# Summing gathered weights with two 64-column products per token, and a last scaling that reads its norm from PSUM

## The chip, the cores and the metric

The kernel runs on one core of a Trainium2 chip. A core has five engines that run side by side and meet at semaphores: PE (TensorE, matrix products, with its weight loads PEld), DVE (VectorE), ACT (ScalarE), POOL (GpSimd) and SP (SyncE, which here only issues transfers). Data come from HBM into SBUF by DMA; PE writes its results into PSUM. The metric is the time of one execution on the device in microseconds (us), lower is better.

## The reference, cut to what matters

One layer of a decoder trunk is run on 512 prompt tokens and 64 sample tokens (D = 2048). After a mixer come eight heads of a product-key lookup ("PEER"): for every token and head the best 16 of 16384 small experts are chosen, and their outputs are summed with weights.

```python
top, pos = lax.top_k(cand, PEER_TOPK)
eidx = jnp.take_along_axis(cidx, pos, axis=-1)
g = jax.nn.softmax(top, axis=-1)
act = jax.nn.gelu(jnp.einsum('td,thkd->thk', xb, expert_u[eidx])) * g
out = jnp.einsum('thk,thkd->td', act, expert_v[eidx])
...
x = x + gate2 * out
y = rmsnorm(x, final_g)        # x / sqrt(mean(x^2) + eps) * final_g
```

The outputs are y for both groups of tokens and the recurrent states of the mixer.

## The kernel before

**Stages.** The first 960 us hold the mixer; then come the queries, keys and choices of the experts. From 1207 us on the kernel walks through the experts themselves. Each expert number is a pair (row, column) of a 128x128 grid. The 80 rows of the grid that are chosen most (`L = 80`) are done densely for all 512 prompt tokens; picks in the other rows are fetched one row of 8 KB at a time with indirect DMAs ("gathers") and dotted on VectorE.

**The u stage (L1645 to L1722).** It has 160 halves, `n = 0..159`, two for each dense row. `u_half` (L1388) issues 24 products of 128x128 weights with 512 columns (L1398). ACT and POOL have split the weights into a high and a low part before (`xhi` L925, `xlo` L926), from `raw` tiles that SP loads some halves ahead. Among these the loop places, for each half, what belongs to the rest: a few gathers of u rows (POOL L1234) with their dot products (DVE L1262, whose second operand `hT` lies in PSUM), steps of the choice, and, from about n = 54 on, the weights' table.

**The weights' table ("Gather's sums").** The dense part needs, for each token, the 128 columns by 80 rows of its softmax weights. For four tokens (`b`) `g_pair` (DVE L1585) makes, per token, two one-hot matrices over the token's 128 picks: `op` (128 picks x 128 columns, scaled by ACT in `g_scale`, L1593) and `wr` (128 picks x 80 rows). `g_mm` (L1595) multiplies the two on PE, so that each token's sum of weights stands in PSUM as 128x80. `g_out` (ACT L1606) copies four tokens out to `stg`, and for each 32 tokens four transfers of 320 KB (`gd<-stg`, POOL L1611) bring it to HBM. `g_eight` (L1632) does two `b` at a time, into the banks `gbank` and `gx`: 64 such blocks in all. One stands either before a `u_half` (odd n) or in its middle (`mid`, even n). Nothing else of PE runs inside a block. In `g_mm` each token's 128 output partitions are cut into four slices of 32, each a product of its own on 32 columns of the array.

**The order.** The engines run in the order in which the code issues (`manual_schedule`); each engine has one queue.

**The v stage and the end.** From 2240 us on the dense v rows are multiplied (L1421, `v_column`), and gathered v rows are added (DVE L1290). The last group adds, per chunk k of 16 (128 channels x 512 tokens), the gathered tokens by four transposing products (L1425), then `v_sum` (L1438) scales by `gate2` on DVE (L1445), squares on ACT (L1449), stores a copy (`x2d`, SP L1450) and adds the squares on DVE (L1455). After k = 15 `token_norm` (L1457) sums the squares on PE (L1463), takes the root (`rstd`, L143 to L149), and spreads the result over the partitions with PE into the PSUM bank `prfa` (L1468); ACT copies it to SBUF as `R` (L1470). Then the 16 chunks are scaled by `R` and `final_g` (L1811 to L1819): 11 on DVE in one operation, 5 (k = 2, 5, 8, 11, 14) first on ACT, then on POOL. SP stores each chunk to `y`. A fallback (L1825 on) follows that runs only when a count overflows.

Of the kernel before, what the change touches and what calls it, by code (L numbers as in the profile page):

```python
# [9 lines left out]
AF = mybir.ActivationFunctionType  # L10
ALU = mybir.AluOpType
# [5 lines left out]
KD = 16  # L17
# [13 lines left out]
NA = NP  # L31
NG = T - NA
NE = 128
L = 80
# [38 lines left out]
C_FG = 232  # L73
# [7 lines left out]
def build(ctx, tc, A, O, dbg=None):  # L81
    nc = tc.nc
    V, S, PE, G = nc.vector, nc.scalar, nc.tensor, nc.gpsimd
# [11 lines left out]
    cols = const.tile([128, C_ALL], F32, name="cols")  # L95
# [117 lines left out]
    def square_sum(src, k, st, nm):  # L213

        if k == 0:
            st.append(wk.tile([128, T], F32, name=f"sqa_{nm}", tag="R", bufs=1))
            S.activation(st[0], src, AF.Square)
# [7 lines left out]
    def norm_stats(st, n, nm):  # L225
# [7 lines left out]
        def spread():  # L233
            out = nm != "n1" and wk.tile([128, T], F32, name=f"R_{nm}", tag="R", bufs=1)
            pr = [pst.tile([128, 512], F32, name=f"st_{nm}_{i}", tag="st") for i in range(2)]
            for i in range(4):
                PE.matmul(pr[0][:, i * 128:(i + 1) * 128], c[:, 0, i:i + 1].to_broadcast([128, 128]), ident,
                          start=True, stop=True)
            PE.matmul(pr[1][:, :64], c[:, 0, 4:5].to_broadcast([128, 128]), ident[:, 64:], start=True, stop=True)
            if nm == "n1":  # L240
                return pr[0], pr[1][:, :64]
            S.activation(out[:, :NP], pr[0], AF.Copy)
            S.activation(out[:, NP:], pr[1][:, :64], AF.Copy)
            return out
# [19 lines left out]

    def modulate(src, R, jscale, jshift, k0, nk, nm):

        sc, sh = mods[jscale], mods[jshift]
        for k in range(k0, k0 + nk):
            m = wk.tile([128, NP], F32, name=f"m_{nm}_{k}", tag="sq", bufs=2)
            hi, lo = hv[0][:, k, :NP], hv[1][:, k, :NP]  # L270
            if R is None:
                V.tensor_scalar(m, src[:, k, :NP], sc[:, k, 0:1], sh[:, k, 0:1], op0=ALU.mult, op1=ALU.add)
                S.activation(hi, src[:, k, :NP], AF.Identity, scale=sc[:, k, 0:1], bias=sh[:, k, 0:1])
                (G if k % 2 else V).tensor_sub(lo, m, r32(hi))
            else:
                V.tensor_mul(m, src[:, k, :NP], R[:, :NP])
                S.activation(hi, m, AF.Identity, bias=sh[:, k, 0:1])
                V.scalar_tensor_tensor(lo, m, sh[:, k, 0:1], r32(hi), op0=ALU.add, op1=ALU.subtract)
        kk = slice(k0, k0 + nk)
        m = wk.tile([128, nk, NB * NS], F32, name=f"ms_{nm}_{k0}", tag="ms", bufs=1)  # L280
        eng = V if R is None else G
        if R is None:
            V.tensor_tensor(s4(m), s4(src[:, kk, NP:T]), ctx_b(sc, kk), op=ALU.mult)
        else:
            eng.tensor_mul(m, src[:, kk, NP:T], R[:, None, NP:T].to_broadcast([128, nk, NB * NS]))
        eng.tensor_tensor(s4(m), s4(m), ctx_b(sh, kk), op=ALU.add)
        split(hv[0][:, kk, NP:T], hv[1][:, kk, NP:T], m, eng)
# [47 lines left out]
    for hc in range(4):  # L335
# [11 lines left out]
        for kq in range(4):  # L347
# [3 lines left out]
            if hc == 0 and kq == 0:  # L351
                R = spread()
# [213 lines left out]
    for i in range(KW):  # L566
# [6 lines left out]
        if i == 0:  # L573
            R = spread()
# [18 lines left out]
    R = spread()  # L593
# [33 lines left out]
    R = spread()  # L627
# [226 lines left out]
    for i in range(RB):  # L854
        r, k = new_row(f"row0_{i}")
# [522 lines left out]
    fin = {}  # L1378
# [55 lines left out]
    def add_x(q, kq):  # L1434
        k = 4 * q + kq
        V.scalar_tensor_tensor(acc[:, k, :], acc[:, k, :], g2[:, k, 0:1], fin["x", q][:, kq, :], op0=ALU.mult, op1=ALU.add)

    def v_sum(gi, k, pv):  # L1438
        ak = acc[:, k, :]
        if gi == 0:  # L1440
            S.activation(ak, pv, AF.Copy)
        elif gi < len(GROUPS) - 1:
            V.tensor_add(ak, ak, pv)  # L1443
        else:
            V.scalar_tensor_tensor(ak, pv, g2[:, k, 0:1], ak, op0=ALU.mult, op1=ALU.add)  # L1445
            if k == 0:
                fin["t"] = [actp.tile([128, NA], F32, name=f"sqs{i}", tag="act") for i in range(3)]
            sq = fin["t"][1]
            S.activation(sq, ak, AF.Square)  # L1449
            nc.sync.dma_start(x2d[:, k, :], ak)  # L1450
            if k == 0:
                fin["sq"] = fin["t"][0]
                V.tensor_copy(fin["sq"], sq)
            else:
                V.tensor_add(fin["sq"], fin["sq"], sq)  # L1455

    def token_norm(sq, n, nm, pool, banks):  # L1457

        nt = -(-n // 128)
        w = min(128, n)  # L1460
        pc, pr = banks
        for i in range(nt):
            PE.matmul(pc[:w, i:i + 1], sq[:, i * 128:i * 128 + w], ones[:, 0:1], start=True, stop=True)  # L1463
        c = pool.tile([128, 3, nt], F32, name=f"rcf{nm}")
        rstd(c[:w, 0, :], pc[:w, :nt], D, c[:w, 1, :], c[:w, 2, :])
        yield
        for i in range(nt):
            PE.matmul(pr[:, i * 128:i * 128 + w], c[:w, 0, i:i + 1].to_broadcast([w, 128]), ident[:w, :w], start=True, stop=True)  # L1468
        R = fin["t"][2] if nm == "a" else pool.tile([128, n], F32, name=f"Rf{nm}")
        S.activation(R, pr[:, :n], AF.Copy)  # L1470
        yield
        return R

# [121 lines left out]
    def g_mm(b, pg):  # L1595
        ops, wr, j0 = pair.pop(b)
        for j in range(4):
            for a in range(0, 128, 32):
                PE.matmul(pg[a:a + 32, j * L:(j + 1) * L], ops[:, j0 + j, a:a + 32], wr[:, j0 + j, :],  # L1599
                          start=True, stop=True)  # L1600

    def g_out(b, pg):
# [121 lines left out]
    vp = ctx.enter_context(tc.tile_pool(name="vp", bufs=1, side="right"))  # L1724
    acc = vp.tile([128, KD, NA], F32, name="acc")
# [39 lines left out]
    for m in range(M):  # L1765
        gi, q, bl, first, final = steps[m]
        n = NU2 + 2 * m
# [12 lines left out]
        for kq in range(KD // VQ):  # L1780
# [9 lines left out]
            k, pv = v_column(n, gi, q, bl, first, final, kq)  # L1790
# [9 lines left out]
    def drive(gen):  # L1800
        while True:
            try:
                next(gen)
            except StopIteration as e:
                return e.value

    def norm_banks(nm):
        return pbank("u", f"pcf{nm}", 2), pbank("g", f"prf{nm}", 2)

    R = drive(token_norm(fin["sq"], NA, "a", vp, norm_banks("a")))  # L1810
    for k in range(KD):  # L1811
        ak = acc[:, k, :]
        fg = cols[:, C_FG + k:C_FG + k + 1]
        if k % 3 == 2:
            S.activation(ak, ak, AF.Copy, scale=fg)
            G.tensor_mul(ak, ak, R)
        else:
            V.scalar_tensor_tensor(ak, ak, fg, R, op0=ALU.mult, op1=ALU.mult)
        nc.sync.dma_start(O["y"][:, k, :NA], ak)  # L1819


    epx.close()
# [2 lines left out]
    with tc.If(any_ > 0), tc.tile_pool(name="fb", bufs=1) as fp:  # L1825
        io1 = fp.tile([128, 128], F32, name="f_io1")
        V.tensor_scalar(io1, iota, 1.0, None, op0=ALU.add)
        for i, (p0, n, c) in enumerate(GT):
# [19 lines left out]
            a = fp.tile([128, D], F32, name=f"f_a{i}", tag="a", bufs=1)  # L1848
# [33 lines left out]
        R = drive(token_norm(sqs, NA, "f", fp, norm_banks("f")))  # L1882
# [72 lines left out]
```

## Time and profile before

| | us |
|---|---|
| median of 3 runs (lowest, highest) | 3210.41 (3208.57, 3221.06) |
| the profiled execution's own time | 3213.08 |
| its span, first to last instruction | 3211.3 |
| PE / DVE / POOL / ACT busy | 3042.5 / 2228.9 / 1796.5 / 1041.5 |
| bytes moved by DMA | 881.12 MB |

The profile is of one execution. Its rows name a line of the kernel, an engine, an operation, what it writes and reads (out<-in), and how often it ran; then busy time, mean duration in ns, and idle time just before it with the releaser that ended most of it. "PE" rows are matrix products, "PEld" rows the loads of their weights. An fp32 product of the program appears as two pairs of records, one load and one product each: `g_eight` has 32 products, and 64 product records in the trace. "SPq" and the like are the issuing of transfers, not their movement.

### The profile page before, as it was taken

To read this page: it belongs to the slowest core of one execution; us is meant where nothing else is said; L and a number is where in the kernel's file an instruction comes from. 1 tells how busy PE (TensorE), PEld (TensorE's weight loads), DVE (VectorE), ACT (ScalarE), POOL (GpSimd) and SP (SyncE) were. 2 spreads that over 40 slices of the span, in tenths; PEclk is the share of its full clock that TensorE was granted. 3 is DMA by queue.
4 is the path that set the end of the run, shared out by engine and by line. 5 is a ranking of instruction groups with operands and counts; after the bars stand their busy time and mean duration, and the time that the engine had idled before them with its cause. 6 is when DMAs were issued, how large, how long until landed. Compare 5 with 4: busy or idle time off the path is not lost.

```text
span 3211.3 us, 52705 instructions
## 1 busy us (share of the span) xinstructions
PE 3042.5 (95%) x20313; PEld 2569.5 (80%) x20313; DVE 2228.9 (69%) x3296; ACT 1041.5 (32%) x1645; POOL 1796.5 (56%) x1097
## 2 busy tenths in 40 slices
PE   5999999999989999999999999999999999999997
PEld 2688798899979998886777777777887778777776
DVE  5356521234356797988899888877679898878955
ACT  3243311123232223232665555542322222222222
POOL 2233233344333335665676676777777778777842
PEclk8999999999989999999999999999999999999998
DMA  9833465633332226989889998998999998999964
GB/s 373 295 136 135 163 216 204 210 115 117 130 134 101 70 77 216 314 323 358 331 303 341 358 385 324 396 369 341 392 411 411 410 377 299 374 384 360 378 202 144
DMA packets 251057, 881.12 MB, mean 274 GB/s; under 512 B 36230, under 2 KB 37126, under 8 KB 194342
## 3 DMA queue, kind: packets, MB, share of 16 engines
q0 software_dynamic: 78096, 475.29, 37.5%
q1 hardware_dynamic: 161760, 382.48, 33.8%
q10 hardware_dynamic: 10944, 19.93, 1.6%
q8 instruction: 160, 2.62, 0.3%
q14 instruction: 97, 0.79, 0.1%
HBM read 878.84 MB, written 65.76 MB: 294 GB/s over the span
## 4 chain that ended last, share of the span: by engine, by line
PE 76%; DMA 10%; DVE 6%; issue 4%; POOL 2%; ACT 1%; SPq 0%; POOLq 0%; DVEq 0%; ACTq 0%
PE pu L1398 24%; PE pv L1421 17%; PE pp_o L139 6%; DMA raw<-vq 3%; PE pp_s L139 3%; PE pp_c L139 3%; PE pp_x L139 3%; PE qb L139 3%; PE pp_b L139 3%; DMA v<-v,rows 2%; PE ada L189 2%; PE pp_y L139 2%; PE qa L139 2%; DMA wa<-w_ada 2%; PE gx L1599 2%
## 5 line engine op out<-in xcount | busy, mean ns | idle before, releaser
L926 POOL TENSOR_TENSOR xlo<-raw,xhi 128x1024 fp32r<-128x1024 f32 x320 | 785.5, 2464 | 395.9 <-ACT xhi L925 391.5
L1262 DVE SCALAR_TENSOR_TENSOR u<-u,hT 128x2048 f32<-128x2048 f32 x223 | 504.9, 2283 | 142.1 <-DMA u<-u,rows 124.0
L925 ACT ACTIVATE xhi<-raw 128x1024 fp32r<-128x1024 f32 x320 | 338.3, 1060 | 760.0 <-PE pv L1421 282.8
L1290 DVE SCALAR_TENSOR_TENSOR accB<-v,dots,accB 128x2048 f32<-128x2048 f32 x211 | 496.4, 2352 | 124.1 <-DMA v<-v,rows 120.4
L1421 PE MATMUL pv<-ahi,xhi 128*128 128x512 f32 x1280 | 507.0, 396 | 30.6 <-DVE acc L1443 26.7
L1398 PE MATMUL pu<-hhi,xhi 128*128 128x512 f32 x1280 | 507.4, 396 | 0.7 <-ACT qt L949 0.7
L1398 PE MATMUL pu<-hhi,xlo 128*128 128x512 f32 x1280 | 499.3, 390 | 6.3 <-POOL xlo L926 6.3
L1421 PE MATMUL pv<-alo,xhi 128*128 128x512 f32 x1280 | 503.4, 393 | 1.1 <-DVE alo L1372 1.1
L1421 PE MATMUL pv<-ahi,xlo 128*128 128x512 f32 x1280 | 503.3, 393 | 0.1
L1398 PE MATMUL pu<-hlo,xhi 128*128 128x512 f32 x1280 | 499.2, 390 | 0.0
L1421 PEld LDWEIGHTS pv<-ahi,xhi 128*128 128x128 f32 x1280 | 243.8, 190 | 85.9 <-issue 16.0
L1234 POOL DMA_INDIRECT v<-v,rows x223 | 260.5, 1168 | 63.2 <-issue 44.8
L1398 PEld LDWEIGHTS pu<-hhi,xlo 128*128 128x128 f32 x1280 | 240.6, 188 | 58.6 <-POOL xlo L926 7.5
L1398 PEld LDWEIGHTS pu<-hhi,xhi 128*128 128x128 f32 x1280 | 240.5, 188 | 57.6 <-issue 1.7
L1421 PEld LDWEIGHTS pv<-ahi,xlo 128*128 128x128 f32 x1280 | 243.3, 190 | 52.4 <-POOL xlo L926 1.0
L1421 PEld LDWEIGHTS pv<-alo,xhi 128*128 128x128 f32 x1280 | 244.0, 191 | 51.5 <-DVE alo L1372 1.5
L1234 POOL DMA_INDIRECT u<-u,rows x223 | 226.8, 1017 | 97.2 <-DVE u L1262 46.2
L1398 PEld LDWEIGHTS pu<-hlo,xhi 128*128 128x128 f32 x1280 | 240.9, 188 | 47.8
L1593 ACT ACTIVATE op<-op,it 128x128 f32<-128x128 f32 x512 | 155.2, 389 | 0.0
L128 POOL TENSOR_TENSOR wlo_q<-raw_q,whi_q 128x1024 fp32r<-128x1024 f32 x28 | 68.7, 2456 | 147.1 <-ACT whi_q L126 147.1
L189 PE MATMUL ada<-wa,cpad 128*32 128x512 f32 x768 | 109.8, 669 | 40.6 <-DMA wa<-w_ada 40.6
L1401 ACT ACTIVATE act<-pu 128x512 f32<-128x512 f32 x80 | 47.9, 598 | 295.3 <-PE pu L1398 291.1
(506 smaller groups left out, 5687.2 us busy)
## 6 DMA issues: line engine op xcount, KB each, us to landing
wa<-w_ada SPq DMA_DIRECT2D x96, 1024.0 KB
raw<-ut SPq DMA_DIRECT2D x160, 512.0 KB
raw<-vq SPq DMA_DIRECT2D x320, 256.0 KB
gd<-stg POOLq DMA_DIRECT2D x64, 320.0 KB
gsb<-gd POOLq DMA_DIRECT2D x20, 1024.0 KB
actd<-act ACTq DMA_DIRECT2D x76, 256.0 KB
actr<-actd POOLq DMA_DIRECT2D x19, 1024.0 KB
raw_o<-w_out SPq DMA_DIRECT2D x32, 512.0 KB
```

The costliest lines, as they stand in the source:

```text
L128: lo_engine(share).tensor_sub(lo, raw, r32(hi))
L139: PE.matmul(o, st, mv[pick](k), start=first, stop=last)
L189: PE.matmul(acc[32 * g:32 * g + 32, :], cpad[:, 4 * kq + g, :], w[:, g, :], start=kq == 0, stop=kq == 3)
L925: S.activation(hi, raw, AF.Copy)
L926: G.tensor_sub(lo, raw, r32(hi))
L1234: G.indirect_dma_start(out=out, out_offset=None, in_=src, in_offset=bass.IndirectOffsetOnAxis(ap=idx, axis=0), bounds_check=NE * 128 - 1, ...
L1262: V.scalar_tensor_tensor(r, r, 1.0, st["h"], op0=ALU.mult, op1=ALU.mult, accum_out=dots[i][:, j:j + 1])
L1290: V.scalar_tensor_tensor(st["a"], r, dots[i][:, j:j + 1], st["a"], op0=ALU.mult, op1=ALU.add)
L1398: PE.matmul(pu, st[:, kk, :], movA[mv](k), start=k == 0 and a == 0, stop=k == KD - 1 and a == 2)
L1421: PE.matmul(pv, st, mv, start=first and j == 0 and a == 0, stop=last and not end and j == SG - 1 and a == 2)
L1593: S.activation(ops[:, j0 + j, :], ops[:, j0 + j, :], AF.Copy, scale=it[2][:, b * 4 + j:b * 4 + j + 1])
L1599: PE.matmul(pg[a:a + 32, j * L:(j + 1) * L], ops[:, j0 + j, a:a + 32], wr[:, j0 + j, :], start=True, stop=True)
```

## The change

Three edits. First, `g_mm` cuts the 128 output partitions of a token into two slices of 64, not four of 32: two products per token on 64 columns of the array each, with the same 80 moving columns. Second, the five chunks that POOL scales at the end are now k = 1, 4, 7, 10, 13, and ACT multiplies them by `final_g` inside `v_sum`, three chunks after each is complete (two for k = 13). Third, `R` is copied from PSUM by DVE, not ACT; DVE's own 11 chunks read the norm straight from the PSUM bank, and only POOL reads the copy; ACT's queue, not SP's, stores POOL's five chunks.

```diff
+    scaled_early = (1, 4, 7, 10, 13)
     def v_sum(gi, k, pv):
...
                 V.tensor_add(fin["sq"], fin["sq"], sq)
+            e = k - 2 if k == KD - 1 else k - 3
+            if e in scaled_early:
+                S.activation(acc[:, e, :], acc[:, e, :], AF.Copy, scale=cols[:, C_FG + e:C_FG + e + 1])
...
         R = fin["t"][2] if nm == "a" else pool.tile([128, n], F32, name=f"Rf{nm}")
-        S.activation(R, pr[:, :n], AF.Copy)
+        if nm == "a":
+            V.tensor_copy(R, pr[:, :n])
+        else:
+            S.activation(R, pr[:, :n], AF.Copy)
...
         for j in range(4):
-            for a in range(0, 128, 32):
-                PE.matmul(pg[a:a + 32, j * L:(j + 1) * L], ops[:, j0 + j, a:a + 32], wr[:, j0 + j, :],
+            for a in range(0, 128, 64):
+                PE.matmul(pg[a:a + 64, j * L:(j + 1) * L], ops[:, j0 + j, a:a + 64], wr[:, j0 + j, :],
                           start=True, stop=True)
...
-    R = drive(token_norm(fin["sq"], NA, "a", vp, norm_banks("a")))
+    banks = norm_banks("a")
+    R = drive(token_norm(fin["sq"], NA, "a", vp, banks))
     for k in range(KD):
         ak = acc[:, k, :]
-        fg = cols[:, C_FG + k:C_FG + k + 1]
-        if k % 3 == 2:
-            S.activation(ak, ak, AF.Copy, scale=fg)
+        if k in scaled_early:
             G.tensor_mul(ak, ak, R)
+            nc.scalar.dma_start(O["y"][:, k, :NA], ak)
         else:
-            V.scalar_tensor_tensor(ak, ak, fg, R, op0=ALU.mult, op1=ALU.mult)
-        nc.sync.dma_start(O["y"][:, k, :NA], ak)
+            V.scalar_tensor_tensor(ak, ak, cols[:, C_FG + k:C_FG + k + 1], banks[1][:, :NA], op0=ALU.mult, op1=ALU.mult)
+            nc.sync.dma_start(O["y"][:, k, :NA], ak)
```

The first place is PE's queue around the first block of the table, in the u stage. Before, each bank takes 16 products with weights of 32 columns:

```order
L1398 MATMUL pu_14112<-hlo,xhi_13977 128x512
L1398 MATMUL pu_14112<-hhi,xlo_13978 128x512
L1599 MATMUL gbank<-wr_13884,op_13883 32x80 x16
L1599 MATMUL gx_14125<-wr_13884,op_13883 32x80 x16
L1398 MATMUL pu_14112<-hhi,xhi_13977 128x512
```

Now it takes 8 with 64 columns, at the same place:

```order
L1398 MATMUL pu_14112<-hlo,xhi_13977 128x512
L1398 MATMUL pu_14112<-hhi,xlo_13978 128x512
L1607 MATMUL gbank<-wr_13884,op_13883 64x80 x8
L1607 MATMUL gx_14125<-wr_13884,op_13883 64x80 x8
L1398 MATMUL pu_14112<-hhi,xhi_13977 128x512
```

Nothing around the blocks moves on any engine: the block has half as many products.

The second place is ACT's queue at the end of the program, from the last weight splits (`xhi`) on. `sqs` is the square of a chunk, `rcfa` the column of norms, `acc` the chunks. Before:

```order
L925 ACTIVATE xhi_29536<-raw_29332 128x1024
L1449 ACTIVATE sqs_29360<-acc 128x512 x8
L144 ACTIVATE rcfa<-rcfa 128x4
L1470 ACTIVATE sqs_29361<-prfa 128x512
L1815 ACTIVATE acc<-acc,cols 128x512 x5
L1823 TENSOR_LOAD flag
```

Now:

```order
L925 ACTIVATE xhi_28514<-raw_28308 128x1024
L1451 ACTIVATE sqs_28336<-acc 128x512 x3
L1460 ACTIVATE acc<-acc,cols 128x512
L1451 ACTIVATE sqs_28336<-acc 128x512 x3
L1460 ACTIVATE acc<-acc,cols 128x512
L1451 ACTIVATE sqs_28336<-acc 128x512 x2
L1460 ACTIVATE acc<-acc,cols 128x512
L144 ACTIVATE rcfa<-rcfa 128x4
L1824 DMA y<-acc 128x512 x5
L1831 TENSOR_LOAD flag
```

The five scalings by `final_g` have gone from behind the root (L144) to between the squares, the copy of `R` has left ACT, and five stores have come to its queue. DVE has the copy in its place, ahead of its 11 chunks:

```order
L149 TENSOR_TENSOR rcfa<-rcfa 128x4
L1476 COPY sqs_28337<-prfa 128x512
L1826 SCALAR_TENSOR_TENSOR acc<-acc,cols,prfa 128x512 x11
L1831 TENSOR_LOAD flag
```

SP's queue keeps 11 of its 16 stores of `y`.

## The prediction

> **What bounds the kernel now.** I read the page first: busy shares, then the chain that ended last.
>
> ```profile
> PE 3042.5 (95%) x20313; PEld 2569.5 (80%) x20313; DVE 2228.9 (69%) x3296; ACT 1041.5 (32%) x1645; POOL 1796.5 (56%) x1097
> PE 76%; DMA 10%; DVE 6%; issue 4%; POOL 2%; ACT 1%; SPq 0%; POOLq 0%; DVEq 0%; ACTq 0%
> ```
>
> PE is busy for 95% of the span and is 76% of the chain; what shortens PE's own work shortens the kernel, as long as nobody else becomes late. "issue", 4%, is waiting that no other engine explains. The change works in two stretches, so I asked for windows: the stretch with the weights' table (1527 to 2140 us), the v stage, and one with the densest transfers.
>
> ```profile
> core 0: us, PE busy (x) PEld busy (x) DVE busy (x) ACT busy (x) POOL busy (x), PEclk, DMA share, GB/s
> 1527.00:2140.00 613.00, 594.06 (x6223) 473.23 (x6223) 529.34 (x727) 349.24 (x769) 427.59 (x308) 1.00 0.91 349
> 2240.00:3100.00 860.00, 828.11 (x3599) 680.42 (x3598) 712.71 (x400) 205.40 (x192) 649.53 (x407) 0.98 0.94 367
> 2027.00:2077.00 50.00, 48.35 (x495) 38.47 (x494) 40.56 (x39) 27.92 (x62) 35.28 (x26) 1.00 1.02 413
> ```
>
> In the table's stretch PE idles 613.00 - 594.06 = 18.9 us, at full granted clock (1.00). The groups by line of that stretch say where:
>
> ```profile
> L1599 PE MATMUL gx<-wr,op 128*32 128x80 f32 x2048 | 65.3, 234 | 18.9 <-issue 18.9
> L1599 PE MATMUL gbank<-wr,op 128*32 128x80 f32 x2048 | 48.7, 236 | 0.0
> ```
>
> All idle time of PE here stands ahead of products into `gx`, the second bank of a block, none ahead of `gbank`, the first. The two banks get the same 2048 products, yet `gx` takes 65.3 + 18.9 = 84.2 us and `gbank` 48.7. PE's rows in order of time show two of the 64 blocks:
>
> ```profile
> 1874.30 0.76 PE L1599 MATMUL gbank<-wr,op 128*32 128x80 f32 x32
> 1874.88 0.74 PE L1599 MATMUL gx<-wr,op 128*32 128x80 f32 x18
> 1876.01 0.35 PE L1599 MATMUL gx<-wr,op 128*32 128x80 f32 x4 [0.39 <-issue]
> 1876.76 0.35 PE L1599 MATMUL gx<-wr,op 128*32 128x80 f32 x5 [0.40 <-issue]
> 1877.53 0.36 PE L1599 MATMUL gx<-wr,op 128*32 128x80 f32 x5 [0.42 <-issue]
> 1877.81 0.50 PE L1398 MATMUL pu<-hhi,xhi 128*128 128x512 f32 x1
> ...
> 1886.20 0.76 PE L1599 MATMUL gbank<-wr,op 128*32 128x80 f32 x32
> 1886.78 0.74 PE L1599 MATMUL gx<-wr,op 128*32 128x80 f32 x32
> 1887.44 0.50 PE L1398 MATMUL pu<-hhi,xhi 128*128 128x512 f32 x1
> ```
>
> The later block is clean: 64 products in 1.24 us. The earlier one runs at the same pace for 32 + 18 = 50 products and then gets only four or five every 0.75 us, so that it takes 3.51 us. The many small products outrun something that feeds PE or takes its records away. The trace does not name it; it shows when it bites: late in a block, never within the first 32 products (the idle time 0.0 of `gbank` covers all 64 blocks). The earliest I found:
>
> ```profile
> 1586.18 0.76 PE L1599 MATMUL gbank<-wr,op 128*32 128x80 f32 x32
> 1586.76 0.45 PE L1599 MATMUL gx<-wr,op 128*32 128x80 f32 x12
> ```
>
> Here 44 went through, then came a pause. The 3.51 us block starts 0.77 us after POOL issued a transfer of the table:
>
> ```profile
> 1873.53 0.92 POOL L1611 DMA_DIRECT2D gd<-stg  x1
> ```
>
> **The change part by part.** *Stalls in the blocks.* A clean `gx` half is 0.74 us, so 64 of them are 47.4; they took 84.2, so stalls cost 84.2 - 47.4 = **36.8 us**. After the change a block has 32 product records, not 64: as many as the half that never stalls. I take all 36.8 as removed. The bounds are 0 (what feeds PE is slow for a time, not after a count) and 36.8.
>
> *The clean block.* Does it get shorter or longer? Eight groups of four slices fill `gbank` in 1886.78 - 1886.20 = 0.58 us, 0.072 us a group. The nearest rows for a stream in fp32 are the transposing products near the end, and for weight loads with next to no stream the sums of squares:
>
> ```profile
> 3172.85 1.05 PE L1425 MATMUL pv<-ident,tok 128*128 128x128 f32 x8
> 3172.62 1.08 PEld L1425 LDWEIGHTS pv<-ident,tok 128*128 128x128 f32 x8
> ...
> 3187.13 0.97 PEld L1463 LDWEIGHTS pcfa<-ones,sqs 128*128 128x128 f32 x8 [2.54 <-issue]
> ```
>
> Less a tail of some 0.2 us, eight products with 128 moving columns come every 0.11 us; 80 columns scale to 0.069. So a group of four slices takes what one slice's stream takes: the slices run side by side and the stream is the limit. Two slices of 64 stream the same 80 columns in as many groups (8 a bank), so the block keeps its 1.24 us. The load doubles in columns. L1463 loads 128 columns every 0.112 us ((0.97 - 0.19)/7, 0.19 being one load), so 64 take 0.056, less than the stream's 0.069, and L1425 shows a load of 0.11 lying wholly beside a stream of 0.11. I take 0 for the clean block; the bounds are 0 and the slower rival's price, below.
>
> [...] So the saving lies in the stalls.
>
> *What lies beside.* With 36.8 us less, the stretch lasts 576 us, and the others must do their work in it. DVE's 529.3 us are 92% of that. DMA moved 349 GB/s x 613 us = 214 MB, which needs 371 GB/s; the window at 2027 us held 413. What DVE and SP's loads waited for in this stretch:
>
> ```profile
> DVE u L1262 <- DMA u<-u,rows: 74.7, 53, 4.9
> ...
> SPq L909 <- POOL xlo L926: 529.4, 90, 9.0
> ```
>
> SP's loads wait for buffers to come free, not for bandwidth, so they have slack; DVE's 74.7 us of waiting for gathered rows say that gathers are near their limit in places. If DMA can't rise above the 0.94 of the v stage, the stretch shrinks only to 613 x 0.91 / 0.94 = 593, and 17 of the 36.8 are given back. If the 1.02 of the dense window holds, nothing is. Nearer to the latter, as that is the same stage: I take **5 us given back**, bounds 0 and 17.
>
> *The end.* After the last products, in order of time:
>
> ```profile
> 3184.82 0.75 DVE L1445 SCALAR_TENSOR_TENSOR acc<-pv,mod,acc 128x512 f32<-128x512 f32 x1 [1.43 <-PE pv L1425]
> 3185.66 0.63 ACT L1449 ACTIVATE sqs<-acc 128x512 f32<-128x512 f32 x1 [2.99 <-DVE acc L1445]
> ...
> 3191.81 0.60 ACT L1470 ACTIVATE sqs<-prfa 128x512 f32<-128x512 f32 x1 [3.19 <-PE prfa L1468]
> 3192.30 3.16 ACT L1815 ACTIVATE acc<-acc,cols 128x512 f32<-128x512 f32 x5
> 3192.44 12.46 DVE L1818 SCALAR_TENSOR_TENSOR acc<-acc,cols,sqs 128x512 f32<-128x512 f32 x11 [2.81 <-ACT sqs L1470]
> 3193.09 7.94 POOL L1816 TENSOR_TENSOR acc<-acc,sqs 128x512 f32<-128x512 f32 x5 [29.82 <-ACT acc L1815]
> 3193.22 13.53 SPq L1819 DMA_DIRECT2D y<-acc  x16
> ```
>
> DVE's 11 chunks set the pace of the stores. Groups of two short windows, with POOL at work and without it, and a group of an operation with one input in PSUM:
>
> ```profile
> L1818 DVE SCALAR_TENSOR_TENSOR acc<-acc,cols,sqs 128x512 f32<-128x512 f32 x4 | 6.8, 1760 | 0.0
> ...
> L1818 DVE SCALAR_TENSOR_TENSOR acc<-acc,cols,sqs 128x512 f32<-128x512 f32 x5 | 3.4, 740 | 0.0
> ...
> L1262 DVE SCALAR_TENSOR_TENSOR u<-u,hT x223: 2269/2283/2291, 1250.7 to 2203.5; 128x2048 f32<-128x2048 f32 x112
> ```
>
> With both tensor inputs in SBUF a chunk takes 1760 ns beside POOL and 740 alone. L1262, whose `hT` lies in PSUM, spreads by only 22 ns over 223 runs, though POOL works through much of that time. So with the norm in PSUM all 11 run at about 3.4/5 = 0.68 us: 7.5 us, not 12.46, and DVE ends 5.0 us earlier. The stores don't keep up with that:
>
> ```profile
> 3193.00:3203.00 10.00, 0.00 (x0) 0.00 (x0) 10.00 (x9) 2.46 (x5) 7.94 (x5) 0.50 0.57 208
> 3203.00:3208.00 5.00, 0.00 (x0) 0.00 (x0) 1.90 (x3) 0.00 (x0) 0.00 (x0) 0.50 1.03 381
> ```
>
> The 16 x 256 KB = 4.19 MB need 11.0 us at 381 GB/s. Begun at 3194.3, a microsecond after the first issue, they land by 3205.3; before, 2.08 and 1.90 MB had gone by 3208, and the rest landed at about 3208.6. Gain 3.3 us. DVE's copy of the norm starts where ACT's 0.60 us did and is bounded by that and the 0.75 of L1445; 0.1 more than ACT's. **The end: 3.2 us**, bounds 0 and 5.0. The five early scalings cost ACT 0.63 each (3.16/5) inside gaps of 2.99 us ahead of its squares: nothing, as long as the stored copy of a chunk has been read within the two or three chunks (7 us or more) before ACT overwrites it; were it late, ACT's next square and DVE behind it would wait, and PE for a bank.
>
> *The sum.* 3213.08 - 36.8 + 5 - 3.2 = 3178.1 for the profiled execution. The median of the runs is 2.7 below it: **3175 us**.
>
> **The rivals.** *The load is not hidden (slower).* [...] As a mechanism of this kernel: if the two 64-column loads of a group run neither beside each other nor beside the streams, a group takes 2 x 0.056 + 0.069 = 0.181 us, not 0.072, and 16 groups in 64 blocks add 112 us: 3210.4 + 112 - 36.8 - 3.2 = 3282. It decides once a group takes over 0.13 us. Against it: four 32-column loads fit into 0.072 us now, and L1425's load lies beside its stream. 5%.
>
> *The stall is one of time.* If the feed turns slow some 0.77 us into a block whatever has run, half as many products wait half as long: 18.4 us saved, 3189. For it: pauses follow transfers of the table. Against it: in the rows above they come after 44 and 50 products, and in `gbank` never. 10%.
>
> *DMA takes over.* At a share of 0.94, 17 us are given back: 3210.4 - 36.8 + 17 - 3.2 = 3187; DVE would then wait more for `u` rows. 10%.
>
> *It doesn't do what it says.* The stalls have another cause and stay: 3207. 7%.
>
> **How the numbers follow.** My forecast has 68%, with 3166 to 3184 of its own (all bounds at their best: 3210.4 - 36.8 - 5.0 = 3169, and 3 for the runs' spread). To leave out no more than 2 in 10, the range reaches to the second and third rivals: 3166 to 3192. About 0.5%, 16 us, is what a measurement of this kernel can tell from no change; 3194 is that line. Forecast, time and DMA rivals lie below it: 0.87 with some loss to spread; stalls that stay lie within: 0.08; slower 0.05.
>
> **What would show it.** In the new profile `gx` has 1024 product records, each with 64 columns, no idle time, and the same busy time as `gbank`; a block takes about 1.24 us; PE's idle time in the stretch is near 0. DVE's chunks at the end take 740 ns beside POOL, and the last window shows DMA near 380 GB/s from its start. Wrong would be: blocks of 2 us or more without pauses (the load), pauses that begin before the 32nd product (time), or new waits of PE for `xlo` in the u stage (DMA).

## The result, and the profile after

The new kernel takes **3182.57 us** (median of 4 runs, 3180.04 to 3183.95), the kernel before beside it 3209.68 (4 runs, 3208.57 to 3221.06): a ratio of 0.9907, with a 95% interval from 0.9892 to 0.9921. The forecast was 3175, between 3166 and 3192. The profiled execution took 3181.82 us, its span is 3179.9.

On other chips, used for the experiments, the kernel before was not always that slow. This turned out to be the main finding, so it stands first:

| where | kernel before, median (runs) | pauses in its blocks | with the change |
|---|---|---|---|
| first occasion (chip not recorded) | 3209.68 (4) | yes | 3182.57, the new kernel |
| chip 10 | 3185.30 (23) | no | 3183.97, its products alone |
| chip 0 | 3185.97 (17) | no | 3180.36, the new kernel |
| chip 12 | 3209.19 (7) | yes | 3178.89, a variant of the new kernel |
| chip 15 | 3213.35 (1) | yes | not run |

Whether there are pauses is read from traces: on chip 0 of the kernel before itself, on chips 10, 12 and 15 of kernels with the same narrow products. The page, and the window that showed 18.9 us of idle PE before:

```profile
PE 3026.1 (95%) x18265; PEld 2566.4 (81%) x18265; DVE 2217.7 (70%) x3297; ACT 1040.1 (33%) x1644; POOL 1793.6 (56%) x1097
...
1527.00:2140.00 613.00, 610.04 (x4290) 495.52 (x4289) 541.59 (x732) 355.08 (x770) 448.01 (x323) 1.00 0.93 365
```

PE has 2048 product records fewer (20313 to 18265) and is busy for 610.04 of 613 us, not 594.06. The groups of PE over all 64 blocks (1520 to 2110 us):

```profile
L1607 PE MATMUL gbank<-wr,op 128*64 128x80 f32 x1024 | 49.9, 239 | 0.0
L1607 PE MATMUL gx<-wr,op 128*64 128x80 f32 x1024 | 46.8, 233 | 0.0
```

Both banks now take about 48 us and nothing is idle ahead of either. Together that is 96.7 us, where it was 48.7 + 65.3 + 18.9 = 132.9. One block in order of time:

```profile
2085.56 0.78 PE L1607 MATMUL gbank<-wr,op 128*64 128x80 f32 x16
2086.16 0.72 PE L1607 MATMUL gx<-wr,op 128*64 128x80 f32 x16
2086.82 0.50 PE L1398 MATMUL pu<-hhi,xhi 128*128 128x512 f32 x1
```

It lasts 2086.82 - 2085.56 = 1.26 us; a clean one lasted 1.24 before. In 0.60 us 16 products start in a bank, where it was 32 in 0.58.

The end, from DVE's last sum on, in order of time, and two windows (columns as before):

```profile
3155.80 0.75 DVE L1447 SCALAR_TENSOR_TENSOR acc<-pv,mod,acc 128x512 f32<-128x512 f32 x1 [1.42 <-PE pv L1425]
...
3163.15 0.69 DVE L1476 COPY sqs<-prfa 128x512 f32<-128x512 f32 x1 [2.23 <-PE prfa L1473]
3163.76 7.32 DVE L1826 SCALAR_TENSOR_TENSOR acc<-acc,cols,prfa 128x512 f32<-128x512 f32 x11
3163.92 6.17 POOL L1823 TENSOR_TENSOR acc<-acc,sqs 128x512 f32<-128x512 f32 x5 [28.83 <-DVE sqs L1476]
```

```profile
3163.00:3168.00 5.00, 0.11 (x1) 0.00 (x0) 4.85 (x8) 0.00 (x0) 4.08 (x4) 0.50 0.55 202
3168.00:3173.00 5.00, 0.00 (x0) 0.00 (x0) 3.08 (x5) 0.00 (x0) 2.09 (x2) 0.50 1.04 379
```

DVE's 11 chunks take 7.32 us, not 12.46, although POOL works beside them for 6.17; from 3168 us on the stores run at 379 GB/s, and they end the work: DVE is done at 3171.1 us, the last of their packets at 3177.4.

Where the 31.4 us between the two profiled spans come from, by the starts of the first and the last block and of DVE's last sum:

| stretch | before | after | difference |
|---|---|---|---|
| up to the first block | 1527.05 | 1523.77 | -3.3 |
| first block to last block | 610.4 | 575.6 | -34.8 |
| last block to DVE's last sum | 1047.3 | 1056.4 | +9.1 |
| DVE's last sum to the end | 26.5 | 24.1 | -2.4 |

The rows are 1527.05 and 2137.48 (`gbank`) and 3184.82 before, 1523.77, 2099.40 and 3155.80 after. The first stretch is before anything that changed; over all fourteen profiled executions of these kernels the first block starts between 1520.2 and 1528.8 us, so -3.3 is scatter. What was given back, 9.1, has a place of its own. The waits of POOL and of PE between 2090 and 2240 us, just behind the blocks, before:

```profile
POOL gsb L1345 <- DMA gd<-stg: 9.8, 1, 9.8
PE pu L1398 <- POOL xlo L926: 4.2, 1, 4.2
```

and after:

```profile
POOL gsb L1345 <- DMA gd<-stg: 10.2, 1, 10.2
PE pu L1398 <- POOL xlo L926: 9.9, 3, 7.0
```

Rows of POOL and then PE, in order of time, after:

```profile
2137.67 1.04 POOL L1234 DMA_INDIRECT u<-u,rows  x1 [0.16 <-issue]
2148.88 0.56 POOL L1345 DMA_DIRECT2D gsb<-gd  x1 [10.16 <-DMA gd<-stg]
2149.45 2.36 POOL L926 TENSOR_TENSOR xlo<-raw,xhi 128x1024 fp32r<-128x1024 f32 x1
...
2151.87 0.79 PE L1398 MATMUL pu<-hhi,xlo 128*128 128x512 f32 x1 [6.97 <-POOL xlo L926]
```

POOL's queue stands for 10 us, because its first load of the finished table (`gsb<-gd`) waits until the last piece has landed in HBM, and the weight split `xlo` behind it starts only then. That wait is as long before as after. A PE that comes later loses 4.2 us to it; one that has not been held up in the blocks loses 9.9. The kernel before, unchanged, on a chip where nothing held it up (chip 0, 2100 to 3165 us), waits longer still:

```profile
PE pu L1398 <- POOL xlo L926: 13.3, 4, 8.5
```

### The profile page after: what moved, and what is told of

It is laid out like the page before. It is cut to its first block, busy times and chain, and to the rows that moved or that the text cites. A ratio compares the mean times of both kernels' runs of the same rounds, so it can differ in the third digit from the quotient of the medians.

```text
span 3179.9 us, 48609 instructions
## 1 busy us (share of the span) xinstructions
PE 3026.1 (95%) x18265; PEld 2566.4 (81%) x18265; DVE 2217.7 (70%) x3297; ACT 1040.1 (33%) x1644; POOL 1793.6 (56%) x1097
## 4 chain that ended last, share of the span: by engine, by line
PE 74%; DMA 12%; DVE 6%; issue 4%; POOL 3%; ACT 0%; SPq 0%; POOLq 0%; DVEq 0%; ACTq 0%
PE pu L1398 25%; PE pv L1421 15%; PE pp_o L139 6%; DMA raw<-vq 5%; DMA v<-v,rows 4%; PE pp_s L139 3%; PE pp_c L139 3%; PE pp_x L139 3%; PE qb L139 3%; PE pp_b L139 3%; PE ada L189 2%; PE pp_y L139 2%; PE qa L139 2%; DMA wa<-w_ada 2%; PE gbank L1607 1%
## 5 line engine op out<-in xcount | busy, mean ns | idle before, releaser
L1234 POOL DMA_INDIRECT u<-u,rows x223 | 226.9, 1017 | 153.9 <-DVE u L1262 103.8
L1234 POOL DMA_INDIRECT v<-v,rows x223 | 253.2, 1135 | 60.6 <-issue 41.2
L128 POOL TENSOR_TENSOR wlo_o<-raw_o,whi_o 128x1024 fp32r<-128x1024 f32 x32 | 77.6, 2426 | 115.9 <-ACT whi_o L126 101.8
```

Source lines behind the costliest of these rows:

```text
L128: lo_engine(share).tensor_sub(lo, raw, r32(hi))
L1234: G.indirect_dma_start(out=out, out_offset=None, in_=src, in_offset=bass.IndirectOffsetOnAxis(ap=idx, axis=0), bounds_check=NE * 128 - 1, ...
```

## The experiments

**The two parts apart** (chip 10). The products alone, on the kernel before:

```diff
-            for a in range(0, 128, 32):
-                PE.matmul(pg[a:a + 32, j * L:(j + 1) * L], ops[:, j0 + j, a:a + 32], wr[:, j0 + j, :],
+            for a in range(0, 128, 64):
+                PE.matmul(pg[a:a + 64, j * L:(j + 1) * L], ops[:, j0 + j, a:a + 64], wr[:, j0 + j, :],
```

> The kernel before, with the 64-column slices alone and the old end. If the gain lies in the stalls of the blocks, as the prediction has it, the blocks of the new kernel account for 35 us of the gain between the two profiled executions, about 6 come back as later waits, and the end is worth 2.4: so 3182.6 + 2.4 = 3185 here, and no idle time ahead of gx. If instead the new end does most of it (fewer stores late, less work of ACT), this one stays above 3195.

and the end alone, that is the new kernel without this edit:

> The kernel before, with the new end alone and four slices of 32. The prediction priced the end at 3.2 us and the new profile shows about 2.4 from the last product's sum to the end of the span: so 3207 against 3209.7 of the kernel before, with the stalls ahead of gx (18.9 us of idle time in the u stage) as they were. Rival: the end gives nothing, because the stores end it either way, 3209.7; or the reads of PSUM beside POOL bring the full 5 us of DVE, 3204.7.

Measured: 3183.97 us (ratio 0.9993, 0.9982 to 1.0005) and 3182.49 (0.9990, 0.9978 to 1.0002), while the kernel before took 3185.30. The first time is the one expected, but for another reason, and the second is 25 us off: here neither part brought anything that these runs can tell from nothing. The kernel with the old products and the new end showed why. Its groups in the blocks:

```profile
L1607 PE MATMUL gbank<-wr,op 128*32 128x80 f32 x2048 | 49.0, 236 | 0.0
L1607 PE MATMUL gx<-wr,op 128*32 128x80 f32 x2048 | 47.6, 233 | 0.0
```

Four slices of 32, 64 product records in a row, and no pause. So the pauses don't follow from the code alone.

**Both kernels once more** (chip 0), unchanged:

> The kernel before, unchanged, profiled on the chip of the other experiments. There its median was 3185.3 us over 23 runs, not 3209.7, and the kernel with four slices of 32 and the new end showed 64 blocks of 1.56 us without a stall. If the stalls belong to the chip or the occasion and not to the code, the trace of this run has no idle time ahead of gx and a time near 3185; if they come and go from run to run, it may show them again, with 3209.

> The new kernel, unchanged, against the kernel before on the same chip. If the gain of 27 us was the stalls, and this chip has none, what remains is the end, 2.4 us, less 0.8 us for 64 blocks that last 1.576 and not 1.563 us: 1.6 us faster, 3183 against 3185. If the chip has the stalls, 3182 against 3210. If the 64 columns bring something apart from stalls, it is faster than 3180 without stalls in the kernel before.

The kernel before showed no pauses again (`gbank` 49.2 us, `gx` 47.6 with no idle time) and took 3190.53 in this run, 3185.97 in the median of 17. The new one took 3180.36: ratio 0.9980 (0.9969 to 0.9991). Without pauses the whole change is worth 0.2%: 5.6 us, by the interval 2.9 to 9.9. The end, 3.0 us as measured below, lies at the lower edge of that; whether the products bring something besides is not shown.

**Twice as many narrow products in a row** (chip 0):

```diff
-            for a in range(0, 128, 32):
+            for a in (*range(0, 128, 32), *range(0, 128, 32)):
```

> The kernel before with each 32-column product of the table issued twice, the second overwriting the first with the same values: 128 product records in a row, in at best 2.4 us a block. If every chip feeds PE only some 50 such records at full pace and then four or five every 0.75 us, a block needs 1.0 + 75/6 = 13 us and the kernel 700 us more; if the feed keeps up with this pace for any count where nothing disturbs it, blocks last 2.6 us without pauses, and the kernel 64 x 1.16 = 74 us more than before on this chip, 3259.

Measured: 3264.69 us, with these groups:

```profile
L1599 PE MATMUL gx<-wr,op 128*32 128x80 f32 x4096 | 85.8, 233 | 5.3 <-issue 5.3
L1599 PE MATMUL gbank<-wr,op 128*32 128x80 f32 x4096 | 85.2, 234 | 1.6 <-issue 1.6
```

Most blocks pass 128 records at full pace. Some 14 of 64 have a single pause, after anything from 16 to 126 records, without a common count. A limit near 50 doesn't exist on this chip.

**The table's transfers, later and in longer runs** (chip 12). Later:

```diff
         if R1 is not None and gk and n % 2 == 0:
             g_eight(n)
+        if R1 is not None and n % 2:
+            put(2)
...
         if R1 is not None:
-            put(1)
```

> The kernel before, with the transfers of the table (gd<-stg) issued two at a time in the middle of each odd half, some 4 us after its block, not one at the start of each half. Only an occasion on which the kernel before stalls (its time near 3209) tells anything: if the stalls need these transfers beside the block, they go or move to the blocks in the middle of even halves, and less than half of the 18.9 us of idle time ahead of gx is left; if the count of records alone does it, idle time and time stay. Where the kernel before has 3185, both expect 3185 here.

In longer runs:

```diff
-    gd = dr.tile([L // SG, 128, NCH, SG * TC], F32, name="gd")
+    gd = dr.tile([4, 128, NCH, L // 4 * TC], F32, name="gd")
...
-                    gd[q // SG:(q + L // 4) // SG, :, c, :].rearrange("s p x -> p s x"),
-                    full[:, q:q + L // 4, :].rearrange("p (s i) t -> p s (i t)", i=SG)))
+                    gd[q // (L // 4), :, c, :],
+                    full[:, q:q + L // 4, :].rearrange("p i t -> p (i t)")))
...
-        G.dma_start(gsb[sg], gd[real_sg[sg]])
+        r, o = divmod(real_sg[sg], L // SG // 4)
+        G.dma_start(gsb[sg], gd[r, :, :, o * SG * TC:(o + 1) * SG * TC])
```

> The kernel before, with the table laid out in HBM so that each of its transfers writes 128 runs of 2560 bytes, not 640 of 512 (the five reads of a run take 512-byte pieces instead). Where the kernel before stalls (near 3209): if the many short writes hold up the feed of PE, idle time ahead of gx falls well under 18.9 us and the time to 3180 to 3200; if not, 3209 stays. Where it has 3185 without stalls, only the reads can show, within 3 us of it.

On this chip the kernel before took 3209.19 us. Issued later: 3200.33. In longer runs: 3224.27. Their `gx` groups, in this order:

```profile
L1601 PE MATMUL gx<-wr,op 128*32 128x80 f32 x2048 | 57.0, 234 | 10.7 <-issue 10.6
```

```profile
L1600 PE MATMUL gx<-wr,op 128*32 128x80 f32 x2048 | 60.0, 234 | 15.2 <-issue 15.2
```

Less the clean 47.4, the pauses cost 20.3 us with later transfers and 27.8 with longer runs, against 36.8 in the profile of before. So later transfers take off 16.5 us. That fits neither reading as it was put: the 10.7 us of idle time are over half of 18.9, and the time is not the old one. But the pauses have not moved with the transfers. Counted from the first block, 15 of the 17 blocks that lose over 0.3 us here are blocks that pause in the profile of before too, and five of the 17 begin 13.5 to 20.8 us behind the last issue of a transfer. What stands beside each of them is something else in POOL's queue: the issue of a gather (`DMA_INDIRECT`, L1234 or L1243). One paused block with later transfers, POOL's rows and then PE's:

```profile
2027.47 1.80 POOL L1613 DMA_DIRECT2D gd<-stg  x2
...
2033.42 1.08 POOL L1234 DMA_INDIRECT u<-u,rows  x1 [0.17 <-issue]
2034.81 1.02 POOL L1234 DMA_INDIRECT u<-u,rows  x1 [0.30 <-issue]
```

```profile
2033.98 0.76 PE L1601 MATMUL gbank<-wr,op 128*32 128x80 f32 x32
2034.56 0.47 PE L1601 MATMUL gx<-wr,op 128*32 128x80 f32 x13
2035.44 0.34 PE L1601 MATMUL gx<-wr,op 128*32 128x80 f32 x4 [0.41 <-issue]
2036.16 0.51 PE L1601 MATMUL gx<-wr,op 128*32 128x80 f32 x15 [0.38 <-issue]
```

And a block of the kernel before, on the first occasion, with a transfer 0.80 us ahead and no gather beside it. It is clean, 1.24 us:

```profile
1557.57 0.93 POOL L1611 DMA_DIRECT2D gd<-stg  x1
1559.45 2.40 POOL L926 TENSOR_TENSOR xlo<-raw,xhi 128x1024 fp32r<-128x1024 f32 x1 [0.94 <-ACT xhi L925]
```

```profile
1558.37 0.76 PE L1599 MATMUL gbank<-wr,op 128*32 128x80 f32 x32
1558.94 0.74 PE L1599 MATMUL gx<-wr,op 128*32 128x80 f32 x32
1559.61 0.50 PE L1398 MATMUL pu<-hhi,xhi 128*128 128x512 f32 x1
```

Counted over all blocks of the two traces there is no exception. In the profile of before POOL begins the issue of a gather in the first 0.9 us of 23 of the 24 paused blocks, 0.01 us ahead of the 24th, and in none of the 40 others (6 of these have one that begins 0.55 to 0.76 us ahead of them). Of 23 blocks with a transfer issued in the 2.5 us ahead of them, the 3 without such a gather are clean; 4 blocks pause with a gather and no such transfer. With later transfers it is 17 of 17 paused blocks and none of 47, and the last pause of each ends 0.28 to 0.46 us behind the end of a gather's issue. So the transfers may matter by their place in POOL's queue, where they hold the gathers back (0.93 us the one at 1557.57, 1.80 us the two at 2027.47): beside the 3.51 us block at 1874.30 two gathers begin 0.45 and 1.80 us behind its start, beside the one at 2033.98, with later transfers, 0.56 us ahead of it and 0.83 us behind, and its pauses are over sooner. That the gathers cause the pauses is not shown, as no run moves them alone, and they don't suffice. On chip 0, where the kernel before runs without pauses, 19 of its blocks have a gather in that place; one of them, POOL's row and then PE's:

```profile
1984.36 1.04 POOL L1234 DMA_INDIRECT u<-u,rows  x1 [0.30 <-issue]
...
1983.91 0.76 PE L1599 MATMUL gbank<-wr,op 128*32 128x80 f32 x32
1984.49 0.74 PE L1599 MATMUL gx<-wr,op 128*32 128x80 f32 x32
```

The 14 single pauses of the doubled narrow products on that chip stand in none of the 13 blocks with such a gather, so they have another cause.

Longer runs lost more than they gained, 15 us in all, which neither reading expected; the loads of the table read them in 512-byte pieces, and PE's waits for ACT and DVE in the v stage were longer (34.0 us for `acc`, not 26.7), but which of these made the loss was not separated.

**64 records at half the pace, and 32 twice** (chip 15). The new kernel with every product issued twice:

```diff
-            for a in range(0, 128, 64):
+            for a in (0, 64, 0, 64):
```

> The new kernel with each 64-column product of the table issued twice, the second overwriting the first with the same values: 64 product records in a block, as before the change, but in twice the time, 2.4 us. Work alone adds 64 x 1.16 = 74 us to the new kernel's 3180: 3254. Where the kernel before stalls (its time near 3209): if the stall comes with the count of records in a row, whatever their pace, it returns after 41 to 62 records in the blocks behind a transfer of the table, for up to 36 us more, 3290; if it comes with the pace (a queue that drains faster than it is filled lasts longer at half the pace), pauses come late in few blocks or not at all, 3254 to 3262. Where the kernel before has 3185, both expect 3254.

And the kernel before with the second half of a block moved six products on, first on chip 10, then here:

```diff
-            for j in range(2):
-                g_mm(b + j, pgs[j])
-            for j in range(2):
-                g_out(b + j, pgs[j])
+            g_mm(b, pgs[0])
+            g_out(b, pgs[0])
+            later.append(lambda: (g_mm(b + 1, pgs[1]), g_out(b + 1, pgs[1])))
...
+            if kk in (2, 6) and later:
+                later.pop()()
```

> The kernel before, with four slices of 32 kept, but the 32 product records of gx moved six products of the u half (1.3 us) behind those of gbank, so that no run of small products is longer than 32. If the stall is one of count (some 44 to 55 records go through at full pace, then the feed is slow), the stalls are gone: no idle time ahead of gx, and the time comes near wide_alone, 3185, plus some 64 x 0.1 us for one more change between kinds of products: 3185 to 3195. If the stall is one of time, or comes from 32-column slices as such, or 1.3 us don't suffice to fill up again, idle time stays ahead of gx or moves ahead of gbank, and the time stays above 3198.

> The kernel before, with its 32-column slices, but the 32 products of gx six products of the u half behind those of gbank (as in blocks_split). Where the kernel before stalls (near 3209): if the stall needs some 41 records in a row, there is none, and the time is that of blocks_split where nothing stalls, 3203, so 6 us below the kernel before in spite of 0.24 us more a block for one more change between kinds of products; if 1.3 us between the halves doesn't suffice to fill up again, pauses stand in the second half, and it takes 3210 or more. Where the kernel before has 3185, it is 3203 as before.

On chip 10, without pauses, the split kernel took 3202.86 us against 3185.30, a loss of 17.6 that was expected at some 6: one more change between kinds of products costs 0.23 us a block, not 0.1 (rows below: 2077.30 - 2076.29 is 1.01 us for a half, two halves less one `u` product of 0.23 make 1.79, where a whole block took 1.56), 14.7 us over 64 blocks. On chip 15, where the kernel before took 3213.35, it took 3214.05, and the doubled one 3261.82. A paused block of the doubled kernel, then one of the split kernel:

```profile
2093.80 1.33 PE L1607 MATMUL gbank<-wr,op 128*64 128x80 f32 x32
2094.95 0.99 PE L1607 MATMUL gx<-wr,op 128*64 128x80 f32 x23
2096.24 0.37 PE L1607 MATMUL gx<-wr,op 128*64 128x80 f32 x4 [0.29 <-issue]
2096.99 0.42 PE L1607 MATMUL gx<-wr,op 128*64 128x80 f32 x5 [0.38 <-issue]
```

```profile
2076.29 0.39 PE L1401 MATMUL pu<-hhi,xlo 128*128 128x512 f32 x1
2076.61 0.76 PE L1602 MATMUL gbank<-wr,op 128*32 128x80 f32 x32
2077.30 0.50 PE L1401 MATMUL pu<-hhi,xhi 128*128 128x512 f32 x1
...
2078.88 0.61 PE L1602 MATMUL gx<-wr,op 128*32 128x80 f32 x21
2079.83 0.47 PE L1602 MATMUL gx<-wr,op 128*32 128x80 f32 x11 [0.34 <-issue]
```

Neither pure reading survives. The pauses return at half the pace, so 64-column slices aren't immune; but they come later and cost less, 87.8 + 7.9 = 95.7 us for `gx` against some 82 clean (`gbank`'s 85.0, less the 3.1 that separate the two banks in the new kernel). And 1.3 us between two halves of 32 do not suffice: a pause stands in the second half. Counted from the start of a block, a paused one gets this far before its first long pause: 50 records in 1.1 us (the block of before at 1874.30), 55 in 1.9 us (32 + 23, doubled), 59 in 2.65 us (32 + 6 + 21, split). About 45 records at once and 5 per us more fit all three, and 4 records every 0.75 us is also what a pause lets through. So, as an estimate from the three, a paused block gets some 45 product records through at full pace and some 5 per us beyond them. `u` products come at 4.4 per us (one each 0.23) and show no such pauses: in the profile of before 0.6 us of idle time stand ahead of them between 1520 and 2145 us, put down to `xlo`. It is no fixed property of the chip: in the profile of before the first long pause comes after 44 to 60 records, and 40 of the 64 blocks pass all their 64 without one. In the doubled and the split kernel too, each paused block (13) and each paused second half (11) has the issue of a gather beside it.

**One product on the whole width** (chip 10):

```diff
-            for a in range(0, 128, 64):
+            for a in range(0, 128, 128):
```

> The new kernel with one product of 128 columns per token, 16 product records in a block. The stream alone would keep a block at 1.24 us and the time at 3182.6, as a group of four slices of 32 and one of two slices of 64 take the same 0.072 us. But a load of 128 columns takes 0.112 us in the sums of squares, more than the stream's 0.069: if products of one column range can't load faster than that, a block lasts 16 x 0.112 = 1.8 us, 0.55 more, and the kernel 64 x 0.55 = 35 us more, 3218. No stalls in either case, with 16 records. A rival: a product on the whole array overlaps the next one less than products on different columns do, which would add to the 35.

Measured: 3198.05 us, ratio 1.0038 (1.0023 to 1.0053) to the kernel before. A block:

```profile
2048.37 1.02 PE L1607 MATMUL gbank<-wr,op 128*128 128x80 f32 x8
2049.23 1.06 PE L1607 MATMUL gx<-wr,op 128*128 128x80 f32 x8
2050.08 0.47 PE L1398 MATMUL pu<-hhi,xhi 128*128 128x512 f32 x1
```

16 products in 1.71 us, 0.107 each: near the pace of a 128-column load (0.112 in the sums of squares), as expected, not that of the stream (0.069, the prediction's estimate from L1425). The time is 20 us below the 3218 that were expected. First to last block take 597.9 us, only 22.3 more than the 575.6 of the new kernel, 0.35 a block and not 0.55: a block takes 1.71 us, not 1.8, and its changes from and to `u` products take 0.1 less than those of blocks with 64 columns (0.23 + 0.31 us, not 0.32 + 0.33, by the starts of PE's records around the two blocks shown). PE's wait for `xlo` behind the blocks is 2.7 us shorter (7.2, not 9.9). With two slices of 64 a group takes 0.60 / 8 = 0.075 us, less than the 0.107 for the same 128 columns in one load, so the two loads don't follow one another at that pace; whether they overlap or are done faster no run tells apart.

**The norm from SBUF** (chip 12): the new kernel, with DVE's last chunks on the copy.

```diff
-            V.scalar_tensor_tensor(ak, ak, cols[:, C_FG + k:C_FG + k + 1], banks[1][:, :NA], op0=ALU.mult, op1=ALU.mult)
+            V.scalar_tensor_tensor(ak, ak, cols[:, C_FG + k:C_FG + k + 1], R, op0=ALU.mult, op1=ALU.mult)
```

> The new kernel, but the 11 last chunks of DVE read the norm from the copy in SBUF that POOL reads, not from PSUM. If the place of that operand is what makes a chunk fast beside POOL, chunks beside POOL take about 1760 ns again, the 11 last some 11 to 12.5 us, not 7.5, and the span ends 2 to 4 us later than the new kernel's at the same distance from the last sum of DVE (24 us there). If POOL's shorter queue is what frees DVE (five products that start at once and end after 6 us), the chunks take 740 ns with either operand, and nothing changes. Where the kernel before has no stalls: 3182 to 3184 by the first, 3180 by the second.

Measured: 3178.89 us, and against the kernel before on its chip 0.9903 (0.9886 to 0.9919). The groups of the end, for this variant and then for the new kernel:

```profile
L1826 DVE SCALAR_TENSOR_TENSOR acc<-acc,cols,sqs 128x512 f32<-128x512 f32 x11 | 12.5, 1207 | 0.0
L1823 POOL TENSOR_TENSOR acc<-acc,sqs 128x512 f32<-128x512 f32 x5 | 7.9, 1616 | 29.3 <-DVE sqs L1476 29.3
```

```profile
L1826 DVE SCALAR_TENSOR_TENSOR acc<-acc,cols,prfa 128x512 f32<-128x512 f32 x11 | 7.3, 739 | 0.0
L1823 POOL TENSOR_TENSOR acc<-acc,sqs 128x512 f32<-128x512 f32 x5 | 6.2, 1271 | 28.8 <-DVE sqs L1476 28.8
```

The place of one operand decides: 12.5 us for DVE's chunks with the norm in SBUF, 7.3 with it in PSUM, and POOL's own products are slower too (1616 and 1271 ns). From DVE's last sum to the end of the span it is 25.6 us, against 23.4 to 24.7 in five profiled executions with the new end (mean 23.9), and 26.3 to 27.4 in eight with the old one (mean 26.9). So of the 3.0 us that the new end brings, some 1.7 are DVE's operand, by this one execution; 2 to 4 were expected. It also keeps the new products on a chip with pauses, and is as much faster there as the new kernel was on the first occasion.

## Why the prediction came out as it did

*Stalls in the blocks, 36.8 us removed.* Right, in place and size: 132.9 - 96.7 = 36.2 us by the groups, no idle time is left, and nothing pauses in either bank. The reason given, that 32 records are as many as the half that never stalled, fits: no paused block of that profile got fewer than 44 records through before its first long pause. What it did not see is that the pauses are not a property of the kernel. Two of the five occasions have none, with the same code, and there this term is zero; and the kernel before is then only 24 us faster, not 36.8: its wait for `xlo` grows from 4.2 to 13.3. The profile of one execution could not show that; the prediction treated 36.8 as a cost of the code.

*The clean block, 0.* Right: 1.26 us, not 1.24, 0.02 x 64, about 1 us. Half as many starts took as long (16 in 0.60 us for a bank, where it was 32 in 0.58), so the number of starts is not what sets the pace.

*What lies beside, 5 us given back.* This step failed, in its mechanism and by half in its size. 9.1 us came back, within the bounds of 0 and 17. The prediction looked for them in DMA's bandwidth and in DVE's gathered rows; PE was busy for 610.04 of 613 us there, with DMA at 365 GB/s and a share of 0.93. They came behind the blocks: 9.9 - 4.2 = 5.7 of them are PE's longer wait for `xlo`, because POOL's queue stands for 10 us ahead of `gsb<-gd`. That `gsb` wait was in the trace before (9.8 us), hidden only because PE was late itself. The list of what would prove the prediction wrong named new waits for `xlo` and put them down to DMA; it was POOL's order. The other 3.4 us are spread over waits of 1 us or so in the v stage and were not traced.

*The end, 3.2 us.* Right: 2.4 in the profiled pair, 3.0 between the means of all executions (26.9 less 23.9). DVE's chunks took 739 ns beside POOL where 680 to 740 was the reading, the stores ran at 379 GB/s, and the stores ended it.

*The sum.* For the profiled execution 3178.1 was forecast and 3181.82 came. By the stretches above the blocks brought 2.0 less than forecast (34.8, not 36.8), the end 0.8 less, and 4.1 more were given back; 3.3 of scatter ahead of the first block went the other way: 3.6 of the 3.7 in all. The median is 7.6 off, as 2.7 was taken off for it, while the new kernel's profiled execution lies 0.75 below its median, not above.

*The rivals.* That the load isn't hidden is wrong with 64 columns (1.26 us a block), and right with 128 (1.71 us, full_width). "The stall is one of time" was priced as half the saving and did not come. Its reason, that pauses follow transfers of the table, was a misreading, and the prediction shared it: the pauses stand beside the gathers that POOL issues behind a transfer, and 3 blocks with a transfer just ahead but no gather have none. In the blocks with a gather the pauses go with the count of records: 22 of the new kernel's blocks, of 32 records, have one in that place, and none of them pauses. DMA did not take over. The 0.13 us a group at which the load was to decide doesn't follow from the prediction's terms: by them the gain of some 35 us is gone at 0.072 + 35 / (16 x 64) = 0.106.

*What stays open.* Why the pauses come on some chips and not on others, what ties them to the gathers, and what holds PE up in them, was not settled. Fetches of instructions from memory are an unlikely cause: in the profile of before they show as queues of their own (kind "instruction": q8, 160 packets of 16 KB, and q14), and 14 of the 24 paused blocks have no such packet under way; for the one at 1874.30 the nearest are at 1866.0 and 1878.4 us. No run tells apart the prediction's two candidates, something that feeds PE and something that takes its records away, and whether the pauses are there when nothing is recorded was not tried. Nor was it tried to keep the gathers away from the narrow blocks, which would show whether they are the cause. Untried, too, is to issue the first `gsb` load from another queue, or later, which is what the 5.7 us above suggest.

## What to carry to other kernels

A stall that the profile puts down to "issue" may belong to the chip: profile the same kernel on a second chip before pricing its removal, and give the gain with and without it. When a stall seems to follow some event, look for the event beside the stretches that don't stall as well: here three clean blocks spoke against the table's transfers. Dense streams of small products should stay short (here under some 45 records in a row, an estimate from three blocks) or be made of fewer, wider products, as long as these don't take longer: here 128 columns took 0.075 us as two product records of 64, and 0.107 as one of 128. When an engine gets faster, look at the fixed waits in the queues of its suppliers: one that was hidden by the old delay, like POOL's 10 us for the last write of the table, is what it meets next.

## What the runs showed of the hardware

- The same code has 36.8 us of pauses on one occasion and none on others, 3209 and 3185 us, at the same granted clock (0.979 and 0.978 for the profiled executions).
- Where it pauses, it does so in the blocks in whose first 0.9 us POOL begins to issue a gather: 24 of 24 (one gather begins 0.01 us ahead), and none of the 40 others, in the profile of before. There PE takes about 45 product records at full pace and some 5 per us beyond (an estimate from three blocks). On a chip without these pauses 50 of 64 blocks pass 128 records without one, in 2.35 us.
- A change between narrow (32 columns) and full-width products cost about 0.23 us for going there and back, by the rows of the split kernel; a block of 16 products with 128 columns takes 1.71 us, 0.107 each.
- One operand in PSUM, not SBUF, takes DVE's 11 last chunks from 1207 to 739 ns in the mean, beside POOL's five products, and these from 1616 to 1271 (one execution each).
